# A head's groups in two parts instead of three, and both parts' later steps behind one product

## The chip, the cores and the metric

The kernel runs on one core of one Trainium2 chip. The metric is the device time of one execution in microseconds (us); lower is better. Everything is float32. The matrix products of the model use the reduced form fp32r three times (high part times high, high times low, low times high) to keep the accuracy; the small products of the attention are plain float32.

## The reference, cut to what matters

One encoder layer over 2048 prompt tokens and 64 sample tokens. After an RMS norm one large projection gives ten streams of 1024 columns. Two branches follow: a gated short convolution, and a gated linear recurrence (8 heads, keys and values of 128). The change touches the recurrence alone:

```python
def hgrn2_block(S, q, k, v, logf):          # one chunk of 64 tokens
    b = jnp.cumsum(logf, axis=1)
    ref = b[:, (L - 1) // 2][:, None]
    att = jnp.where(causal, jnp.einsum('bthk,bshk->bhts', q * jnp.exp(b - ref), k * jnp.exp(ref - b)), 0.0)
    o = jnp.einsum('bhts,bshv->bthv', att, v) + jnp.einsum('bthk,bhkv->bthv', q * jnp.exp(b), S)
    S_new = jnp.exp(b_last)[..., None] * S + jnp.einsum('bshk,bshv->bhkv', k * jnp.exp(b_last[:, None] - b), v)
    return S_new, o
...
    o = o * lax.rsqrt(jnp.mean(o * o, axis=-1, keepdims=True) + EPS)
```

The prompt starts from a zero state, the sample from a given one. The outputs are gated, projected, merged with the other branch, normed, and gated once more.

## The kernel before

The 2112 tokens (the 64 sample tokens stand at position 1344) are cut into three blocks of 704. In each block the kernel runs path B (the recurrence, 8 heads), path A (the convolution branch), then the merge and the output layers.

**Products.** The projections are made by `sgroup` (line 328), which replaces two output tiles' eight half-size block products by seven (`PRODUCTS`), each of 12 matmuls: four blocks of the inner dimension times the three fp32r forms (lines 343, 344 and 345; a 128 x 128 weight against 352 tokens). After each product `hook()` (line 238) takes the next entry of a list and runs it. `None` is an empty turn. In the first block the sums of weight blocks and the low parts of all weights are computed on the way by VectorE (DVE) and written to memory; the later blocks load them.

**A head.** `head_prep` (line 720) makes the forget gate and the queries in one group of seven products, the gate z and the values in a second. On the way ScalarE (ACT) and DVE work out the decays: L727 (sigmoid, from the last of the first seven products), L734 (Ln, with the load of its function table), L736, L737 (the running sum), L739, then exponentials (L748 to L750) and L760 to L765, which end in the keys `kb` (L762). The next head's attention reads these.

**The attention.** Tokens of a block go in groups of 128 (two chunks, called pairs here), and one of 64 at the end: five pairs and one single. `plan()` puts them in three parts: four pairs, one pair, one single. `head_attn` (line 781) is a generator with four steps, for one part:

- step 1: transposes of keys and values (L799, L801) into PSUM, copies to SBUF (ACT, L803, L804), scores (L813, L815), masked copies (DVE, L817, L819);
- step 2: the products keys x values (L825), and the chain of states (DVE, L842, one link per group; L846 for a final state);
- step 3: the outputs (L862 and L864), then their norm: square (ACT, L868), sum (DVE, L869), scale (DVE, L527), power -1/2 (GpSimd, L529, inside `rstd_of`), multiply (DVE, L871);
- step 4: transposes of the outputs (L876) and the multiplication with gate and weight into z (DVE, L878).

`path_b` (line 881) puts these steps into the list of hooks, so a head's attention runs between the 14 products of the next head: step 1 of the three parts after products 1, 2 and 3, step 2 after 4, 5 and 6, step 3 after 7, 8 and 9, an empty turn, step 4 after 11, 12 and 13, and the spill of z to memory after 14.

```python
            for step in range(4):
                hooks.extend(partial(next, g) for g in attn)
                if step == 2:
                    hooks.append(None)
            hooks.append(partial(keep_z, hd, d["z"]))
```

The matmuls of a step are placed right behind the last matmul of the product (`placed()`). On the other engines a scheduler that runs when the program is built sets the order; each engine then works through its queue in that order. One pool of three PSUM banks (`psa`, tiles `pa`) serves the attention, another of five (`psg`, tiles `pg`) the products. The tiles of the parts with one group are called `one` (8 buffers of one group); the four-group tiles come from the large ring `r`.

In the first block every head is followed by one more group of seven products (the branch gates, `gates`); in the other two blocks seven of these eight groups have been made before the heads start.

Of the kernel before, what the change touches and what calls it, by code (L numbers as in the profile page):

```python
# [18 lines left out]
P = 128  # L19
# [4 lines left out]
CH = 64  # L24
# [21 lines left out]
def plan():  # L46
# [3 lines left out]
    for t0 in range(0, TOK, BN):  # L50
# [9 lines left out]
        parts = [groups[i : min(i + 4, npair)] for i in range(0, npair, 4)] + [[g] for g in groups[npair:]]  # L60
# [22 lines left out]
def hybrid_step(  # L83
# [697 lines left out]
    def head_attn(ip, gs, d, hd):  # L781

        nt, ln = len(gs), gs[0]["len"]
        o0, n = gs[0]["off"], nt * ln
        qe, z, att = d["qe"], d["z"], atts[ip]

        def tile3():
            if nt == 1:
                return small.tile([P, 1, P], F32, tag="one", name=nm("one"), bufs=8)
            return cols3(rt(nt * P), nt)  # L790

        def keys(g):
            return d["kb"][:, g["off"] : g["off"] + ln]
# [3 lines left out]
        with placed():  # L797
            for i, g in enumerate(gs):
                T.transpose(p_k[:ln, i * P : i * P + P], keys(g), ident)  # L799
            for i, g in enumerate(gs):  # L800
                T.transpose(p_v[:ln, i * P : i * P + P], d["vt"][:, g["off"] : g["off"] + ln], ident)  # L801
        kt, v = tile3(), tile3()
        A.copy(kt[:ln], cols3(p_k, nt)[:ln])  # L803
        A.copy(v[:ln], cols3(p_v, nt)[:ln])  # L804
        p_a = ps_attn()
        with placed():
            for i, g in enumerate(gs):
                o = g["off"]
                if nt > 1:
                    own, rows = d["ka"][:, o // 2 : o // 2 + P], P  # L810
                else:
                    own, rows = d["ka"][:, o // 2 : o // 2 + CH] if ln == P else keys(g), CH
# [4 lines left out]
        V.copy_predicated(att[:CH, :nt, :ln], caus[:CH, :ln].unsqueeze(1).to_broadcast([CH, nt, ln]), pa3[:CH, :, :ln])  # L817
        if ln == P:
            V.copy_predicated(att[CH:, :nt, CH:], caus[CH:, CH:].unsqueeze(1).to_broadcast([CH, nt, CH]), pa3[CH:, :, CH:])  # L819
# [3 lines left out]
        with placed():  # L823
            for i in range(nt):
                T.matmul(p_u[:, i * P : i * P + P], kt[:ln, i, :], v[:ln, i, :], start=True, stop=True)  # L825
        ss = tile3()
        prevs = []
        sample = gs[0]["sample"]
        if sample:
            cur = small.tile([P, P], F32, tag="s0", name=nm("s0"), bufs=2)  # L830
            G.dma_start(cur, s0[hd])
        else:
            cur = states[hd] if d["carry"] is None else d["carry"]
        for i, g in enumerate(gs):
            u = p_u[:, i * P : i * P + P]
            c = (g["off"] + ln) // CH - 1
# [7 lines left out]
        if g["end"]:  # L844
# [378 lines left out]
```

## Time and profile before

| | |
|---|---|
| median of 3 runs | 2762.88 us (2762.08 to 2769.86) |
| profiled execution, its time | 2764.13 us |
| profiled execution, its span | 2761.8 us |
| TensorE matmuls (PE) | 2683.5 us busy, 97% |
| TensorE weight loads (PEld) | 2608.6 us, 94% |
| VectorE (DVE) | 1718.2 us, 62% |
| ScalarE (ACT) | 1449.9 us, 52% |
| GpSimd (POOL) | 377.3 us, 14% |
| granted TensorE clock | 0.987 |

The span is the time from the first to the last instruction; the time of an execution has some 2 us more. A row of the timeline gives the start in us from the start of the span, the duration of the instructions in the row (several that follow each other are one row, with xN), the engine, the line, the operation, the tile written and the tiles read, the shapes, and in square brackets how long the engine stood idle before, and for what. A float32 matmul of the attention shows as two matmuls (x2), a transpose as one. A matmul's duration overlaps the next one's, so the cost of a stretch is read from start to start. Path B's heads run at about 121 to 480 us (first block), 1117 to 1380 us (second) and 1998 to 2290 us (third).

### The profile page before, as it was taken

What the parts mean: (1) busy time and instruction counts of PE and PEld (TensorE: products, weight loads), DVE (VectorE), ACT (ScalarE), POOL (GpSimd) and SP (SyncE); (2) the same over time, 40 slices, a digit from 0 to 9 for tenths busy, and PEclk for the clock granted to TensorE, in tenths of its full rate; (3) what the DMA queues carried; (4) which work ended last, traced back from release to release, by engine and by line L of the source; (5) the groups of instructions that cost most, each with busy time, mean ns of one, the idle gap of its engine ahead of it and who ended that gap; (6) DMA issues with size and microseconds to landing.
All of it is one profiled execution on the core that took longest, in us unless ns stands there. A gap on an engine that the chain in (4) does not pass through costs nothing.

```text
span 2761.8 us, 47890 instructions
## 1 busy us (share of the span) xinstructions
PE 2683.5 (97%) x16736; PEld 2608.6 (94%) x16736; DVE 1718.2 (62%) x3338; ACT 1449.9 (52%) x2796; POOL 377.3 (14%) x698
## 2 busy tenths in 40 slices
PE   6999999999999999999999999999999999999998
PEld 5999999999999999999999999999999999999988
DVE  6788888899657544455645567453355554357764
ACT  4665565454324554566654555454555554445654
POOL 2000001110332211011111210021000000010022
PEclk7999999999999999999999999999999999999999
DMA  5767767888987898766689998599866668888878
GB/s 199 267 237 272 253 240 277 284 308 292 351 314 274 318 320 272 232 210 214 220 271 335 388 336 261 166 358 305 275 210 207 207 218 261 271 287 303 279 234 314
DMA packets 365553, 748.37 MB, mean 271 GB/s; under 512 B 44704, under 2 KB 48320, under 8 KB 365312
## 3 DMA queue, kind: packets, MB, share of 16 engines
q1 hardware_dynamic: 325728, 589.84, 64.3%
q0 software_dynamic: 39296, 155.44, 15.4%
q8 instruction: 132, 2.16, 0.3%
q14 instruction: 109, 0.89, 0.1%
q10 hardware_dynamic: 288, 0.05, 0.0%
HBM read 537.77 MB, written 207.37 MB: 270 GB/s over the span
## 4 chain that ended last, share of the span: by engine, by line
PE 78%; DMA 8%; issue 4%; DVE 4%; POOL 2%; ACT 1%; DVEq 0%; POOLq 0%; ACTq 0%; SPq 0%
PE pg L343 18%; PE pg L344 17%; PE pg L345 17%; PE pg L436 3%; PE pg L437 3%; PE pg L471 3%; PE pg L438 3%; PE pg L469 3%; PE pg L470 3%; DMA raw<-w_blk 2%; DMA raw<-S 1%; PE pa L825 1%; PE pa L862 1%; PE pa L864 1%; DMA r<-w_blk 1%
## 5 line engine op out<-in xcount | busy, mean ns | idle before, releaser
L343 PE MATMUL pg<-r,hi 128*128 128x352 f32 x3360 | 1116.7, 333 | 12.7 <-ACT r L182 5.9
L344 PE MATMUL pg<-r,hi 128*128 128x352 f32 x3360 | 1089.7, 325 | 4.9 <-DVE r L183 4.9
L213 ACT CAST hi<-raw 128x512 fp32r<-128x512 f32 x740 | 456.0, 619 | 633.2 <-PE pg L344 233.2
L345 PE MATMUL pg<-r,lo 128*128 128x352 f32 x2400 | 779.4, 325 | 5.2 <-DMA lo<-low 4.6
L343 PEld LDWEIGHTS pg<-r,hi 128*128 128x128 f32 x3360 | 633.8, 189 | 31.6 <-ACT hf L359 11.3
L344 PEld LDWEIGHTS pg<-r,hi 128*128 128x128 f32 x3360 | 635.4, 189 | 9.5 <-DVE r L183 9.5
L345 PEld LDWEIGHTS pg<-r,lo 128*128 128x128 f32 x2400 | 453.3, 189 | 7.3 <-DMA lo<-low 6.4
L345 PE MATMUL pg<-r,s 128*128 128x352 f32 x960 | 310.9, 324 | 0.6 <-DMA s<-low 0.6
L469 PE MATMUL pg<-r,hi 128*128 128x352 f32 x896 | 290.8, 326 | 2.7 <-ACT r L182 2.4
L470 PE MATMUL pg<-r,hi 128*128 128x352 f32 x896 | 291.6, 326 | 1.3 <-DVE r L183 1.0
L471 PE MATMUL pg<-r,lo 128*128 128x352 f32 x728 | 237.2, 326 | 7.6 <-DVE lo L183 6.2
L182 ACT CAST r<-r 128x352 fp32r<-128x352 f32 (+2 forms) x294 | 162.9, 589 | 143.1 <-DVE r L962 43.7
L182 ACT CAST hi<-raw 128x512 fp32r<-128x512 f32 (+1 forms) x232 | 138.0, 597 | 188.0 <-PE pg L344 51.7
L183 DVE TENSOR_TENSOR r<-r,r 128x352 fp32r<-128x352 f32 (+2 forms) x294 | 183.5, 649 | 61.9 <-ACT r L182 61.1
L183 DVE TENSOR_TENSOR lo<-raw,hi 128x512 fp32r<-128x512 f32 (+1 forms) x232 | 151.7, 657 | 76.6 <-ACT hi L182 66.3
L436 PE MATMUL pg<-r,hi 128*128 128x352 f32 x560 | 183.0, 331 | 9.3 <-ACT r L182 9.3
L437 PE MATMUL pg<-r,hi 128*128 128x352 f32 x560 | 183.9, 329 | 0.8 <-DVE r L183 0.6
L345 PEld LDWEIGHTS pg<-r,s 128*128 128x128 f32 x960 | 180.6, 188 | 1.0 <-DMA s<-low 0.9
L182 ACT CAST hi<-s 128x512 fp32r<-128x512 f32 x160 | 99.0, 619 | 151.8 <-PE pg L344 146.4
L469 PEld LDWEIGHTS pg<-r,hi 128*128 128x128 f32 x896 | 169.6, 190 | 5.0 <-ACT r L182 3.9
L470 PEld LDWEIGHTS pg<-r,hi 128*128 128x128 f32 x896 | 169.8, 190 | 2.8 <-DVE r L183 2.6
L359 ACT COPY hf<-pg 128x352 f32<-128x352 f32 x360 | 158.3, 446 | 0.5 <-PE pg L345 0.5
(317 smaller groups left out, 3985.1 us busy)
## 6 DMA issues: line engine op xcount, KB each, us to landing
raw<-w_blk SPq DMA_DIRECT2D x588, 256.0 KB, 4.0
lo<-low SPq DMA_DIRECT2D x422, 256.0 KB, 3.9
raw<-S SPq DMA_DIRECT2D x400, 256.0 KB, 4.1
low<-lo SPq DMA_DIRECT2D x344, 256.0 KB, 3.5
s<-low SPq DMA_DIRECT2D x318, 256.0 KB, 3.8
S<-s SPq DMA_DIRECT2D x160, 256.0 KB, 3.2
r<-x_fm POOLq DMA_DIRECT2D x40, 352.0 KB, 6.8
r<-w_blk POOLq DMA_DIRECT2D x48, 256.0 KB, 7.1
```

What stands on the lines that cost most here:

```text
L182: A.copy(hi, src)
L183: V.tensor_tensor(lo, src, hi.bitcast(F32), ALU.subtract)
L213: A.copy(hi, raw)
L343: add(hi[:, k, :], xhi, start=start and k == 0, stop=False)
L344: add(hi[:, k, :], xlo, start=False, stop=False)
L345: last[0] = add(lo[:, k, :], xhi, start=False, stop=k == KH - 1).ins
L359: copied = A.copy(got[n], ps[bank])
L436: add(hi[:, k, :], xhi, start=start and k == 0, stop=False)
L437: add(hi[:, k, :], xlo, start=False, stop=False)
L469: T.matmul(ps, hi[:, k % 4, :], xhi[:, c], start=k == 0, stop=False)
L470: T.matmul(ps, hi[:, k % 4, :], xlo[:, c], start=False, stop=False)
L471: last[0] = T.matmul(ps, lo[:, k % 4, :], xhi[:, c], start=False, stop=k == KB - 1).ins
```

## The change

The parts become two: four pairs, and a pair with the single. Step 1 keeps one turn per part (after products 1 and 2). Steps 2, 3 and 4 run for both parts in one turn: after products 4, 6 and 9; z is spilled after product 10, and the list has ten entries instead of fourteen. Inside `head_attn` the work of the second part, whose groups have different lengths, is done with a pair's instructions and a single's: copies, squares, sums, powers and multiplies keep one instruction for the pair and one for the single (`alike`), in that order; the multiplication into z takes both in one instruction of 192 columns. The second part's tiles hold two groups (`two`, 4 buffers), and the two groups share the PSUM tiles, the tile `on` that takes first the squares and then the normed outputs, and the tile `ms` of sums.

The diff:

```diff
@@ -57,7 +57,7 @@
                     groups.append(dict(off=o, len=min(2 * CH, b - o), sample=sample, first=t0 + o == 0, end=o + 2 * CH >= b))
         npair = sum(g["len"] == 2 * CH for g in groups)
         assert all(g["len"] == 2 * CH for g in groups[:npair])
-        parts = [groups[i : min(i + 4, npair)] for i in range(0, npair, 4)] + [[g] for g in groups[npair:]]
+        parts = [groups[i : i + 4] for i in range(0, len(groups), 4)]
         halves = [dict(t0=t0 + o, off=o, n=HN) for o in (0, HN)]
         out.append(dict(t0=t0, n=BN, runs=runs, npair=npair, parts=parts, groups=groups, segs=halves, last=t0 + BN == TOK))
     return out
@@ -780,60 +780,73 @@
 
     def head_attn(ip, gs, d, hd):
 
-        nt, ln = len(gs), gs[0]["len"]
-        o0, n = gs[0]["off"], nt * ln
+        nt, o0, n = len(gs), gs[0]["off"], sum(g["len"] for g in gs)
         qe, z, att = d["qe"], d["z"], atts[ip]
+        pairs = sum(g["len"] == P for g in gs)
 
         def tile3():
-            if nt == 1:
-                return small.tile([P, 1, P], F32, tag="one", name=nm("one"), bufs=8)
+            if nt == 2:
+                return small.tile([P, 2, P], F32, tag="two", name=nm("two"), bufs=4)
             return cols3(rt(nt * P), nt)
 
+        def alike(*tiles):
+
+            out = [tuple(t[:, :pairs] for t in tiles)] if pairs else []
+            return out + ([tuple(t[:CH, pairs:] for t in tiles)] if pairs < nt else [])
+
         def keys(g):
-            return d["kb"][:, g["off"] : g["off"] + ln]
+            return d["kb"][:, g["off"] : g["off"] + g["len"]]
 
 
         p_k, p_v = ps_attn(), ps_attn()
         with placed():
             for i, g in enumerate(gs):
-                T.transpose(p_k[:ln, i * P : i * P + P], keys(g), ident)
+                T.transpose(p_k[: g["len"], i * P : i * P + P], keys(g), ident)
             for i, g in enumerate(gs):
-                T.transpose(p_v[:ln, i * P : i * P + P], d["vt"][:, g["off"] : g["off"] + ln], ident)
+                T.transpose(p_v[: g["len"], i * P : i * P + P], d["vt"][:, g["off"] : g["off"] + g["len"]], ident)
         kt, v = tile3(), tile3()
-        A.copy(kt[:ln], cols3(p_k, nt)[:ln])
-        A.copy(v[:ln], cols3(p_v, nt)[:ln])
+        for dst, src in alike(kt, cols3(p_k, nt)) + alike(v, cols3(p_v, nt)):
+            A.copy(dst, src)
         p_a = ps_attn()
         with placed():
             for i, g in enumerate(gs):
-                o = g["off"]
-                if nt > 1:
+                o, ln = g["off"], g["len"]
+                if ln < P:
+                    own, rows = keys(g), CH
+                elif pairs > 1:
                     own, rows = d["ka"][:, o // 2 : o // 2 + P], P
                 else:
-                    own, rows = d["ka"][:, o // 2 : o // 2 + CH] if ln == P else keys(g), CH
+                    own, rows = d["ka"][:, o // 2 : o // 2 + CH], CH
                 T.matmul(p_a[:rows, i * P : i * P + CH], own, qe[:, o : o + CH], start=True, stop=True)
                 if ln == P:
                     T.matmul(p_a[:, i * P + CH : i * P + P], keys(g), qe[:, o + CH : o + P], start=True, stop=True)
         pa3 = cols3(p_a, nt)
-        V.copy_predicated(att[:CH, :nt, :ln], caus[:CH, :ln].unsqueeze(1).to_broadcast([CH, nt, ln]), pa3[:CH, :, :ln])
-        if ln == P:
-            V.copy_predicated(att[CH:, :nt, CH:], caus[CH:, CH:].unsqueeze(1).to_broadcast([CH, nt, CH]), pa3[CH:, :, CH:])
+
+        def masked(rows, gr, c):
+            dst = att[rows, gr, c]
+            V.copy_predicated(dst, caus[rows, c].unsqueeze(1).to_broadcast(list(dst.shape)), pa3[rows, gr, c])
+
+        if pairs:
+            masked(slice(0, CH), slice(0, pairs), slice(0, P))
+            masked(slice(CH, P), slice(0, pairs), slice(CH, P))
+        if pairs < nt:
+            masked(slice(0, CH), slice(pairs, nt), slice(0, CH))
         yield
 
         p_u = ps_attn()
         with placed():
-            for i in range(nt):
-                T.matmul(p_u[:, i * P : i * P + P], kt[:ln, i, :], v[:ln, i, :], start=True, stop=True)
+            for i, g in enumerate(gs):
+                T.matmul(p_u[:, i * P : i * P + P], kt[: g["len"], i, :], v[: g["len"], i, :], start=True, stop=True)
         ss = tile3()
         prevs = []
-        sample = gs[0]["sample"]
-        if sample:
-            cur = small.tile([P, P], F32, tag="s0", name=nm("s0"), bufs=2)
-            G.dma_start(cur, s0[hd])
-        else:
-            cur = states[hd] if d["carry"] is None else d["carry"]
         for i, g in enumerate(gs):
+            if g["sample"]:
+                cur = small.tile([P, P], F32, tag="s0", name=nm("s0"), bufs=2)
+                G.dma_start(cur, s0[hd])
+            else:
+                cur = states[hd] if d["carry"] is None else d["carry"]
             u = p_u[:, i * P : i * P + P]
-            c = (g["off"] + ln) // CH - 1
+            c = (g["off"] + g["len"]) // CH - 1
             if g["first"]:
                 prevs.append(None)
                 V.tensor_copy(ss[:, i, :], u)
@@ -841,23 +854,23 @@
                 prevs.append(cur)
                 V.scalar_tensor_tensor(ss[:, i, :], cur, d["f"][:, c : c + 1], u, ALU.mult, ALU.add)
             cur = ss[:, i, :]
-        if g["end"]:
+            if not g["end"]:
+                d["carry"] = cur
+                continue
             end = small.tile([P, P], F32, tag="state", name=nm("state"), bufs=NH + 2)
             V.tensor_scalar(end, cur, d["eq"][:, c * CH + CH - 1 : c * CH + CH], None, ALU.mult)
-            if sample:
+            if g["sample"]:
                 G.dma_start(hgrn_s[hd], end)
             else:
                 states[hd] = end
                 if d["last"]:
                     G.dma_start(hgrn_p[hd], end)
-        else:
-            d["carry"] = cur
         yield
 
         p_o = ps_attn()
         with placed():
             for i, g in enumerate(gs):
-                o = g["off"]
+                o, ln = g["off"], g["len"]
                 dst = p_o[:ln, i * P : i * P + P]
                 T.matmul(dst, att[:ln, i, :ln], v[:ln, i, :], start=True, stop=prevs[i] is None)
                 if prevs[i] is not None:
@@ -865,15 +878,17 @@
         on = tile3()
         ms = small.tile([P, 4], F32, tag="ms", name=nm("ms"))
         po3 = cols3(p_o, nt)
-        A.activation(on[:ln], po3[:ln], AF.Square)
-        V.tensor_reduce(ms[:ln, :nt], on[:ln], axis=mybir.AxisListType.X, op=ALU.add)
-        rstd_of(ms[:ln, :nt], ms[:ln, :nt], 1.0 / P)
-        V.tensor_tensor(on[:ln], po3[:ln], ms[:ln, :nt].unsqueeze(2).to_broadcast([ln, nt, P]), ALU.mult)
+        for dst, src, m in alike(on, po3, ms[:, :nt]):
+            A.activation(dst, src, AF.Square)
+            V.tensor_reduce(m, dst, axis=mybir.AxisListType.X, op=ALU.add)
+            rstd_of(m, m, 1.0 / P)
+            V.tensor_tensor(dst, src, m.unsqueeze(2).to_broadcast(list(dst.shape)), ALU.mult)
         yield
         p_t = ps_attn()
         with placed():
-            for i in range(nt):
-                T.transpose(p_t[:, i * ln : i * ln + ln], on[:ln, i, :], ident[:ln, :ln])
+            for i, g in enumerate(gs):
+                o, ln = g["off"] - o0, g["len"]
+                T.transpose(p_t[:, o : o + ln], on[:ln, i, :], ident[:ln, :ln])
         c = slice(o0, o0 + n)
         V.scalar_tensor_tensor(z[:, c], p_t[:, :n], g_on[:, hd : hd + 1], z[:, c], ALU.mult, ALU.mult)
         yield
@@ -890,11 +905,13 @@
             next(fills, None)
             assert not hooks
             attn = [head_attn(i, gs, d, hd) for i, gs in enumerate(bl["parts"])]
-            for step in range(4):
-                hooks.extend(partial(next, g) for g in attn)
-                if step == 2:
-                    hooks.append(None)
-            hooks.append(partial(keep_z, hd, d["z"]))
+
+            def both(attn=attn):
+                for g in attn:
+                    next(g)
+
+            hooks.extend(partial(next, g) for g in attn)
+            hooks.extend((None, both, None, both, None, None, both, partial(keep_z, hd, d["z"])))
 
 
     def load_p(bl, queue):
```

In the program as built, the matmuls outside the attention stand in the same order as before, and every engine has the same instructions but for 25 fewer on DVE (the multiplication into z, and one memset). The single's square now waits for the pair's multiply, since both use the tile `on` and the PSUM tile. In seven heads of the first block the scheduler put the transpose of the single 33 matmuls behind the transposes of the pairs; in the other 17 heads all six transposes stand together.

## The prediction

> **What bounds the kernel now.** I read the page first, then the busy times of the three stretches of heads, then PE's list of waits.
>
> ```profile
> span 2761.8 us, 47890 instructions
> PE 2683.5 (97%) x16736; PEld 2608.6 (94%) x16736; DVE 1718.2 (62%) x3338; ACT 1449.9 (52%) x2796; POOL 377.3 (14%) x698
> 121.00:480.00 359.00, 357.75 (x2312) 343.07 (x2311) 301.75 (x604) 203.98 (x387) 31.94 (x48) 1.00 0.73 257
> 1117.00:1380.00 263.00, 263.00 (x1738) 250.24 (x1737) 149.99 (x353) 155.79 (x295) 29.36 (x49) 1.00 0.67 216
> 1998.00:2290.00 292.00, 292.00 (x1925) 277.63 (x1924) 161.90 (x371) 165.59 (x316) 26.80 (x43) 1.00 0.68 212
> PE pa L801 <- ACT one L803: 1.5, 1, 1.5
> PE pa L799 <- ACT one L803: 1.4, 1, 1.4
> ```
>
> In the stretches (window; its length; then busy PE, PEld, DVE, ACT, POOL; clock; DMA) PE is busy without a hole: 357.75 of 359 us, 263 of 263, 292 of 292, at full clock. So the heads cost what PE's queue costs, and an edit can help only by making that queue shorter or by removing one of PE's few waits. Of the waits, two belong to the attention, 1.5 and 1.4 us, each once. The change can lose by new waits: PE works in order, so a late operand stops everything behind it. DVE is busy for 301.75 us of the first block's 359 (84%), and for 57% (149.99 of 263) in the second: the first block has little room to be late.
>
> **PE's own work.** The number of attention matmuls is unchanged; seven interruptions of the products per head go. What does an interruption cost?
>
> ```profile
> 1221.81 0.33 PE L345 MATMUL pg<-r,s 128*128 128x352 f32 x1
> 1221.97 0.27 PE L876 MATMUL pa<-ident,one 128*128 128x128 f32 x1
> 1222.00 0.41 PE L343 MATMUL pg<-r,hi 128*128 128x352 f32 x1
> 1222.25 0.33 PE L344 MATMUL pg<-r,hi 128*128 128x352 f32 x1
> ...
> 1235.55 0.32 PE L345 MATMUL pg<-r,s 128*128 128x352 f32 x1
> 1235.71 0.27 PE L799 MATMUL pa<-ident,r 128*64 128x128 f32 x1
> 1235.82 0.27 PE L801 MATMUL pa<-ident,r 128*64 128x128 f32 x1
> 1236.02 0.33 PE L813 MATMUL pa<-r,r 128*64 128x64 f32 x2
> 1236.28 0.43 PE L343 MATMUL pg<-r,hi 128*128 128x352 f32 x1
> 1236.55 0.32 PE L344 MATMUL pg<-r,hi 128*128 128x352 f32 x1
> ```
>
> Read from start to start, a matmul of a product takes 0.16 us (1221.81 to 1221.97). One full transpose between products moves the second matmul behind it to 1222.25, that is 0.44 us after 1221.81 where two matmuls alone take 0.32: 0.12 us. The same operation inside a row of its kind takes 0.11 (1235.71 to 1235.82). So an interruption as such costs 0.01 us, since the 0.25 at its end (1222.00 to 1222.25) is given back by the 0.03 before it. 168 interruptions fewer (7 x 24 heads) bring 0 to 2 us; I take 1.
>
> The 64-wide pieces do cost a change: the scores of the single start 0.20 after the transpose ahead of them instead of 0.11 (1235.82 to 1236.02). The merged step 1 has two such places, as the two clusters have now: the pair's narrow L813 and the single's. In steps 2 to 4 the single's 64-row matmuls keep one way in and one way out. I take 0, between 1 us less and the bound of the second rival.
>
> [...]
>
> The two waits of 1.5 and 1.4 us are the third part's transposes waiting for the second part's copies on ACT; that turn is empty now, and step 2 comes a product later: 2.9 us less.
>
> **The new lateness: the single's norm.** Step 3 to step 4 was four products and is now three. And the single's norm no longer runs beside the pair's: its square waits for the pair's multiply, so square, sum, scale, power and multiply run twice in a row. I work it out from one head of the first block, with time 0 at the start of the square of the four pairs.
>
> ```profile
> 343.96 0.39 PE L864 MATMUL pa<-r,r 128*128 128x128 f32 x2
> ...
> 348.59 0.43 PE L862 MATMUL pa<-one,att 64*64 64x128 f32 x2
> ...
> 349.31 0.43 PE L343 MATMUL pg<-r,hi 128*128 128x352 f32 x1
> ```
>
> PE: the last output matmul of the four pairs starts at 344.07 (second half of the row at 343.96), 0.32 before time 0 (row 344.39 below). Then the pair's four halves (0.11 each, 0.45), the single's way in (0.20) and its work (0.72, 348.59 to 349.31): the next product starts 1.36 after 344.07. Three products are 36 x 0.16, with 0.09 more at the first: 5.85. So the transposes start 7.2 after 344.07, at 6.9. In blocks two and three the single's comes behind five others (0.54) and its way in (0.1): needed at 7.55. In seven heads of the first block 33 matmuls stand between (5.3, with 0.2 at both ends): needed at 12.9.
>
> ```profile
> 342.83 0.52 DVE L383 TENSOR_TENSOR hf<-hf,pg 128x352 f32<-128x352 f32 x1 [0.31 <-PE pg L345]
> 343.38 0.50 ACT L727 ACTIVATE r<-hf 128x352 f32<-128x352 f32 x1
> 344.39 0.60 ACT L868 ACTIVATE r<-pa 128x512 f32<-128x512 f32 x1 [0.51 <-PE pa L864]
> 345.69 1.28 ACT L734 ACT_TABLE_LOAD   x1
> 346.51 0.16 DVE L527 TENSOR_SCALAR ms<-ms 128x4 f32<-128x4 f32 x1
> 346.82 1.04 POOL L529 TENSOR_TENSOR ms<-ms,mhalf 128x4 f32<-128x4 f32 x1 [20.85 <-DVE ms L527]
> 346.98 0.98 ACT L734 ACTIVATE r<-r,lbt 128x704 f32<-128x704 f32 x1
> 347.90 0.69 DVE L871 TENSOR_TENSOR r<-pa,ms 128x512 f32<-128x512 f32 x1 [1.22 <-POOL ms L529]
> 348.50 0.64 DVE L736 TENSOR_SCALAR r<-r,lbt 128x704 f32<-128x704 f32 x1
> 349.06 1.62 DVE L737 TENSOR_TENSOR_SCAN r<-keep,r 128x704 f32<-128x704 f32 x1
> 350.59 1.26 DVE L183 TENSOR_TENSOR lo<-raw,hi 128x512 fp32r<-128x512 f32 x2
> 351.78 0.88 DVE L739 TENSOR_TENSOR r<-r 128x704 f32<-128x704 f32 x1
> 352.58 0.46 DVE L869 TENSOR_REDUCE ms<-one 128x1 f32<-128x128 f32 x2
> 352.97 0.67 DVE L183 TENSOR_TENSOR lo<-s,hi 128x512 fp32r<-128x512 f32 x1
> 353.57 0.20 DVE L527 TENSOR_SCALAR ms<-ms 128x1 f32<-128x1 f32 x2
> 353.69 0.67 DVE L279 TENSOR_TENSOR s<-s,raw 128x512 f32<-128x512 f32 x1
> 355.31 0.28 DVE L871 TENSOR_TENSOR one<-pa,ms 64x128 f32<-64x128 f32 x1 [0.20 <-POOL ms L529]
> 362.38 0.73 DVE L878 SCALAR_TENSOR_TENSOR r<-pa,vec,r 128x512 f32<-128x512 f32 x1
> ```
>
> The four pairs' multiply ends at 4.2, as before (347.90 + 0.69 - 344.39). Behind it in the built order stand the pair's L527 and L383 (0.52, on the seventh product, which now follows step 3): 4.7.
>
> Blocks two and three: scale to multiply takes 1.39 with a power of 1.04 (346.51 to 347.90); for the two small groups, one after the other, it takes 1.74 (353.57 to 355.31), so 0.9 is taken for one. The pair is multiplied from 5.0 to 5.3; then the single's square (taken as 0.3, as its sum and multiply), sum 0.3, scale to multiply 0.9, multiply 0.3: 7.0 to 7.1. Needed at 7.55: hidden, with 0.5 us to spare, behind the three products. I take 0. If each of the chain's ten hand-overs takes 0.1 longer, it costs 0.5 in each of the 16 heads.
>
> First block: L727 (0.50) waits for L383 and the Ln's table load (1.28) and Ln (0.98) follow: Ln ends at 7.5, where it ended at 3.6 before (346.98 + 0.98 - 344.39). On DVE the built order behind it is L736, L737, two L183, the single's sum, L739, L183, the single's scale, the four pairs' L878, L279, the single's multiply. From start to start in the rows: 0.56, 1.53, 1.19, 0.20, 0.80, 0.60, 0.08, 0.66, 0.60 and 0.28 for the last: 6.5. The multiply ends at 14.1, the transpose wants it at 12.9: PE stands for about 1.25 us, queued behind it the rest of the product and all later ones. In seven heads 8.8 us. The ends are 0 (if Ln comes a microsecond earlier) and 2.2 a head (15 us; if a cast that a L183 waits for is late by one more).
>
> **What else is late.** The exponentials and the keys follow Ln. In the first block seven gate products still stand between (84 matmuls, 13 us) and cover the 3.9 us. In blocks two and three the keys are done well ahead:
>
> ```profile
> 1261.26 0.48 DVE L762 TENSOR_TENSOR r<-hf,qc 128x320 f32<-128x320 f32 x1
> 1265.39 0.60 PE L799 MATMUL pa<-ident,r 128*128 128x128 f32 x4
> ```
>
> 3.65 us. The three output steps that stood behind the seventh product (3.1 us of PE: 16 halves at 0.11 and the 1.36 worked out above) now stand ahead of it, and Ln comes about as long after that product as before. By that 0.5 us is left. Hidden, at 0; without that cover each microsecond costs 16. Step 3 after step 2 is two products (3.9 us) and the chain of six states takes some 2 us: hidden. The spill of z is issued earlier on POOL, behind nothing that it waited for before.
>
> **Sum.** -1 (interruptions) + 0 (mode changes) - 2.9 (two waits) + 8.8 (first block) + 0 (blocks two and three) = +4.9. The profiled execution took 2764.1 (span 2761.8 and 2.3 around it), 1.25 above the median 2762.9 of the runs; with the change 2769.0 by the profile, 2768 against the median. What a measurement of this kernel can tell from no change is about 0.3%, 8.3 us: so I forecast no change that can be told, on the slow side.
>
> **Rivals.**
>
> *The serial norm is late in every head* (slower). Place: the single's transpose. If the chain is 1 us longer than worked out, blocks two and three lose 0.5 in 16 heads (8) and the first block 2.25 in seven (16): +20, 2783. It passes 8.3 us from a lengthening of 0.5 us: 7 x 1.75 - 3.9. For it: ten hand-overs between four engines, and DVE's 84%. Against: the durations repeat from head to head. 0.22.
>
> *Each change of tile width drains* (slower). Step 1 would go to narrow tiles and back once more. One such trip costs 0.24: from 1235.55 to 1236.55 is 1.00, less two matmuls of a product (0.32) and the four pieces at 0.11 (0.44). 0.24 x 24 = 5.8 on top: +10.7, 2774. Against: row 1235.71, a 64-wide transpose that starts 0.16 behind a full matmul, and the next 0.11 behind it, so transposes pay nothing. [...] 0.08.
>
> *An interruption costs a fixed price* (faster). If the 0.09 of the first matmul behind each (0.25 instead of 0.16) were a net cost, 168 fewer save 15 us: 2753. Against: the 0.12 worked out above. [...] 0.05.
>
> *The change does nothing that shows*: no head waits, as the scheduler left 33 matmuls for it. -3.9: 2759. 0.20.
>
> **Numbers.** Forecast 0.45, of it 0.36 inside 0.3% and 0.09 above. Same: 0.36 + 0.18 (nothing shows; 0.02 of it faster) + 0.04 (norm late) + 0.02 = 0.60. Slower: 0.09 + 0.18 + 0.06 = 0.33. Faster: 0.02 + 0.05 = 0.07. The range goes from 2757 (no new waits, the two old ones gone, 2 less for interruptions, and a margin of 1 us) to 2781 (15 us in the first block, 6 in the others, less 3).
>
> **What would show it.** PE waits in the first block at the transpose of the single (tile `two`) for DVE's multiply, seven times about 1.2 us; none in blocks two and three; the two waits for L803's copies gone; clusters as long as their parts were. It is wrong if PE has waits at the pairs' transposes, at step 2 or 3, or at the next head's first transposes, or if the products between clusters are no longer 0.16 apart.

## The result, and the profile after

The change makes the kernel slower. Its median is 2778.97 us (2776.59 to 2783.8, six runs) against 2762.82 (2761.1 to 2769.86, six runs) of the kernel before: a ratio of 1.0056, 95% interval 1.0043 to 1.0069. That is 16 us, inside the range of 2757 to 2781, but twice the 8.3 us (0.3%) that the prediction took as the bound of what can be told, and had forecast it to stay under. The profiled execution took 2783.8 us, 19.7 more than that of before; its span is 20.3 longer.

Two rows of the page after, for the span and the engines:

```profile
span 2782.1 us, 47864 instructions
PE 2686.9 (97%) x16736; PEld 2623.0 (94%) x16736; DVE 1721.9 (62%) x3313; ACT 1452.6 (52%) x2796; POOL 374.7 (13%) x698
```

No engine has more work to speak of. The busy times by stretch (columns as in the prediction) show where the time is: first before, then after.

```profile
150.00:500.00 350.00, 347.27 (x2239) 332.94 (x2238) 295.85 (x598) 196.26 (x374) 32.07 (x49) 1.00 0.74 260
```

```profile
150.00:500.00 350.00, 329.42 (x2065) 318.38 (x2066) 279.30 (x547) 184.06 (x343) 24.50 (x39) 0.98 0.71 240
1140.00:1420.00 280.00, 280.00 (x1851) 269.04 (x1850) 157.90 (x370) 163.10 (x314) 30.70 (x51) 1.00 0.68 217
2030.00:2310.00 280.00, 280.00 (x1839) 269.21 (x1838) 160.50 (x358) 160.66 (x301) 26.60 (x43) 1.00 0.66 210
```

In blocks two and three PE is busy without a hole, as before. The loss is in the first block's heads: PE stands still for 20.6 of 350 us there (2.7 before), and the granted clock is 0.98. PE's waits in the first block's heads (what waits, for what; total us, times, longest) are two rows:

```profile
PE pg L343 <- DVE hf L364: 13.6, 7, 2.0
PE pa L891 <- DVE two L885: 7.5, 7, 1.1
```

The second row is the wait that the prediction priced: the single's transpose, seven times. The first row is new and was not in it. L364 is an addition on DVE that reads a bank of the products' PSUM pool; until it has run, the bank isn't free and the next product of the gate group can't start. The two waits for the copies of the old L803 are gone.

### The profile page after: what moved, and what is told of

Read it like the earlier page. It is cut to its first block, busy times and chain, and to the rows that moved or that the text cites. A ratio compares the mean times of both kernels' runs of the same rounds, so it can differ in the third digit from the quotient of the medians.

```text
span 2782.1 us, 47864 instructions
## 1 busy us (share of the span) xinstructions
PE 2686.9 (97%) x16736; PEld 2623.0 (94%) x16736; DVE 1721.9 (62%) x3313; ACT 1452.6 (52%) x2796; POOL 374.7 (13%) x698
## 4 chain that ended last, share of the span: by engine, by line
PE 79%; DMA 6%; DVE 5%; issue 4%; POOL 1%; ACT 1%; DVEq 0%; POOLq 0%; SPq 0%; ACTq 0%
PE pg L343 18%; PE pg L344 18%; PE pg L345 18%; PE pg L436 3%; PE pg L437 3%; PE pg L438 3%; PE pg L471 3%; PE pg L469 3%; PE pg L470 3%; DMA raw<-w_blk 2%; DMA lo<-low 2%; PE pa L839 1%; PE pa L875 1%; PE pa L877 1%; PE pa L820 1%
## 5 line engine op out<-in xcount | busy, mean ns | idle before, releaser
L343 PE MATMUL pg<-r,hi 128*128 128x352 f32 x3360 | 1106.8, 330 | 23.6 <-DVE hf L364 13.6
L183 DVE TENSOR_TENSOR r<-r,r 128x352 fp32r<-128x352 f32 (+2 forms) x294 | 183.5, 649 | 62.3 <-ACT r L182 61.4
L183 DVE TENSOR_TENSOR lo<-raw,hi 128x512 fp32r<-128x512 f32 (+1 forms) x232 | 151.9, 658 | 81.0 <-ACT hi L182 71.6
```

The source lines that it names most:

```text
L183: V.tensor_tensor(lo, src, hi.bitcast(F32), ALU.subtract)
L343: add(hi[:, k, :], xhi, start=start and k == 0, stop=False)
```

## Where the new wait comes from

One head of the kernel after (timeline; rows as explained above): rows of ACT and DVE first, then rows of PE.

```profile
362.24 0.98 ACT L734 ACTIVATE r<-r,lbt 128x704 f32<-128x704 f32 x1
...
368.19 0.73 DVE L893 SCALAR_TENSOR_TENSOR r<-pa,vec,r 128x512 f32<-128x512 f32 x1
369.45 0.28 DVE L885 TENSOR_TENSOR two<-pa,ms 64x128 f32<-64x128 f32 x1
370.46 0.41 DVE L893 SCALAR_TENSOR_TENSOR r<-pa,vec,r 128x192 f32<-128x192 f32 x1
...
376.41 0.88 DVE L765 TENSOR_TENSOR r<-r,qc 128x704 f32<-128x704 f32 x1
377.81 0.51 DVE L364 TENSOR_TENSOR hf<-hf,pg 128x352 f32<-128x352 f32 x1
```

```profile
358.65 0.32 PE L345 MATMUL pg<-r,lo 128*128 128x352 f32 x1
369.78 0.27 PE L891 MATMUL pa<-ident,two 64*128 64x64 f32 x1 [1.08 <-DVE two L885]
378.47 0.40 PE L343 MATMUL pg<-r,hi 128*128 128x352 f32 x1 [1.93 <-DVE hf L364]
```

The same points before, on PE and on DVE:

```profile
342.47 0.32 PE L345 MATMUL pg<-r,lo 128*128 128x352 f32 x1
361.94 0.32 PE L343 MATMUL pg<-r,hi 128*128 128x352 f32 x1
```

```profile
359.94 0.50 DVE L364 TENSOR_TENSOR hf<-hf,pg 128x352 f32<-128x352 f32 x1
360.97 0.87 DVE L765 TENSOR_TENSOR r<-r,qc 128x704 f32<-128x704 f32 x1
362.38 0.73 DVE L878 SCALAR_TENSOR_TENSOR r<-pa,vec,r 128x512 f32<-128x512 f32 x1
```

Time is counted from the start of the last matmul of the seventh product (342.47 before, 358.65 after); 97 matmuls later PE comes to the bank.

- *PE is earlier.* Before, it reaches the bank at 19.47 (361.94). After, at 17.89 (378.47 less 1.93 of waiting): the 22 pieces of the outputs that stood in this stretch now stand ahead of the seventh product, and only the 1.08 at the single's transpose has come in.
- *DVE is later.* Before, L364 ends at 17.97 (359.94 + 0.50), 1.5 us ahead of PE. After, it ends at 19.67 (377.81 + 0.51), 1.8 behind. Ln isn't the cause: it ends at 4.57 after (362.24 + 0.98), where it ended at 5.49 before (346.98 + 0.98 in the prediction's rows). From Ln's end to L364's end DVE needs 15.1 us instead of 12.5. Both multiplications into z and L765 stand ahead of L364 in the built order, where they stood behind it: 1.8 us, from start to start. So do four more operations on the weights, two of L183 and two of L279: 2.3 us. Against them the norms' operations and DVE's own waiting are 1.5 us less.

So 1.5 us to spare became a wait of 1.9. All seven heads have these times to within 0.1 us.

**The wait costs more than its length.** PE behind the same wait in the next head, which lasted 1.95:

```profile
432.18 0.40 PE L343 MATMUL pg<-r,hi 128*128 128x352 f32 x1 [1.95 <-DVE hf L364]
...
432.93 0.49 PE L344 MATMUL pg<-r,hi 128*128 128x352 f32 x1
433.22 0.49 PE L345 MATMUL pg<-r,lo 128*128 128x352 f32 x1
...
436.38 0.32 PE L344 MATMUL pg<-r,hi 128*128 128x352 f32 x1
```

For some 3.5 us the matmuls start 0.29 apart instead of 0.16: the granted clock is 0.50 there (rows of the windows below). Five of the seven waits for L364 are followed by such a stretch, 11 or 12 slow matmuls each, 7.5 us in all; none of the seven waits of 1.1 us is. The five stretches of half clock begin at 159.79, 214.40, 323.63, 432.85 and 487.47 us, last 3.41 us each, and lie 16, 32, 32 and 16 times 3.413 us apart. So in this trace the clock changes at the edges of windows of 3.413 us, and these do not move with PE's waits. Two of these windows and the one behind each, first around the wait at 432.18, then around that at 378.47:

```profile
429.44:432.85 3.41, 1.46 (x9) 1.20 (x9) 3.41 (x7) 1.64 (x3) 0.00 (x0) 1.00 0.76 248
432.85:436.26 3.41, 3.41 (x14) 3.41 (x13) 2.29 (x6) 1.04 (x3) 0.00 (x0) 0.50 0.73 184
374.83:378.24 3.41, 1.71 (x11) 1.41 (x9) 3.41 (x7) 2.53 (x4) 0.00 (x0) 1.00 0.90 338
378.24:381.65 3.41, 3.18 (x20) 3.21 (x21) 3.34 (x8) 1.15 (x3) 0.00 (x0) 1.00 0.76 171
```

The first wait lies whole in one window: PE is busy for 1.46 of its 3.41 us, and the next window has the clock of 0.50. The second is cut by an edge into 1.70 and 0.23, and the clock stays at 1.00.

The sum of the profiled execution: waits for L364 +13.6, slow matmuls behind them +7.5, waits at the single's transpose +7.5, waits for L803 -2.9, interruptions -2.0 (below): +23.7. The span grew by 20.3. Compared at the start of the same matmul of a product, the execution after is 2.7 us ahead before the first attention step (at 119 us) and 23.2 behind past the first block's heads (at 557 us). That is +25.9 in these heads; the terms that fall there give 25.4 (13.6 + 7.5 + 7.5, less 1.5 for L803, 1.0 for five waits for L390 that before has, and 0.7 for a third of the interruptions). So most of the 3.4 that the sum is too high was gained before the change acts, and the change does not explain it.

## The experiments

Each ratio is to the kernel before, timed beside the run (2760.92 to 2761.95 us there). Theory A stands for "VectorE's queue and the place of the outputs", B for "two parts and grouped steps cost TensorE itself"; the other letters are explained in the expectations, where they stand.

**1. L364 first.**

```diff
-                V.tensor_tensor(u2, u2, ps["b"], ALU.add)
+                with tc.high_priority():
+                    V.tensor_tensor(u2, u2, ps["b"], ALU.add)
```

> The changed kernel with one edit: the addition of line 364, which frees a bank of PSUM for the next group of products, is given high priority, so that it stands in VectorE's order behind the first multiply of the outputs instead of behind the keys' and queries' scaling (18 instructions earlier). Theory A (VectorE's order: seven times 2.1 us of the loss are TensorE's wait for that bank, seven times 1.1 us its wait for the single's norm): the waits for line 364 go, -14.7 us; the single's multiply gets up to 1.1 us later in each of the seven heads, 0 to +7.7 us; so 2764 to 2772 us against 2779, ratio to before 1.0005 to 1.0035. Rival B (two parts and steps behind one product cost TensorE time of their own, and the wait at the bank is only where it shows): 2776 to 2780 us, ratio 1.005 to 1.006, the wait shows elsewhere.

2768.86 us, ratio 1.0021 (1.0012 to 1.0031), inside A's range. Its waits in the first block's heads:

```profile
PE pg L343 <- DVE r L391: 7.8, 7, 2.2
PE pa L892 <- DVE two L886: 7.0, 7, 1.0
```

The wait for L364 is gone, and B with it. But a wait of 0.9 has come up (once 2.2) for the next reader of a bank in the same queue, L390 (391 here). The single's wait did not grow, as A had allowed for; but in this program its transpose stands 40 matmuls of the products behind the pairs', 7 more than in the change. With each edit the scheduler places it anew.

**2. Norms abreast.**

```diff
-        for dst, src, m in alike(on, po3, ms[:, :nt]):
+        norms = alike(on, po3, ms[:, :nt])
+        for dst, src, m in norms:
             A.activation(dst, src, AF.Square)
+        for dst, src, m in norms:
             V.tensor_reduce(m, dst, axis=mybir.AxisListType.X, op=ALU.add)
...
```

> The changed kernel with the norms of pair and single written abreast (both squares, both reductions, both powers, both multiplies) instead of one chain after the other. Theory A (one queue: the single's late chain and line 364's late addition both come from VectorE's full order after its idle time for the logarithm): the waits at the single's transpose go, -8.2 us, and as its last links and the multiplies of the outputs now fill the 1.5 us in which VectorE was idle, the addition of line 364 comes 1.5 to 2.5 us earlier and most of its wait goes too, -10 to -14.7 us; so 2756 to 2762 us, ratio 0.9975 to 1.000. Rival C (the serial chain costs its own wait alone; the bank's wait hangs on the logarithm, which is late because the products of the outputs go ahead of the seventh product): -8.2 us alone, 2771 us, ratio 1.003, seven waits of about 2 us for line 364 remain. Rival B (two parts and grouped steps cost TensorE itself): 2776 to 2780 us.

2767.43 us, ratio 1.0015 (1.0007 to 1.0024).

```profile
PE pg L343 <- DVE hf L364: 11.6, 7, 1.8
PE pg L343 <- DVE r L390: 1.9, 7, 0.3
```

The waits at the single's transpose are gone, though it now stands right behind the pairs', without the 33 matmuls between: the serial chain was their cause. L364 still comes late, 1.66 on average instead of 1.94. A missed (2756 to 2762), and C is nearer, with 11.5 us gained instead of its 8.2. The half clock adds to the gain: these waits, 1.59 to 1.76 us, have no slow matmuls behind them.

Why so little of the wait went is seen in one head:

```profile
350.50 0.32 PE L345 MATMUL pg<-r,lo 128*128 128x352 f32 x1
368.20 0.52 DVE L364 TENSOR_TENSOR hf<-hf,pg 128x352 f32<-128x352 f32 x1
368.87 0.40 PE L343 MATMUL pg<-r,hi 128*128 128x352 f32 x1 [1.65 <-DVE hf L364]
```

L364 ends at 18.22 behind the seventh product, 1.45 earlier than in the change, as A had it. But PE comes to the bank at 16.72, 1.2 earlier, since it no longer waits on the way. Before, L364 ended at 17.97 and PE came at 19.47. So in this run the wait is almost all PE's shorter way (2.75 us) and hardly DVE's lateness (0.25). C's reason, a late logarithm, fits this run (Ln ends at 6.75) but not the change (4.57).

**3. Both edits.**

> The changed kernel with both edits: line 364's addition given high priority and the norms of pair and single written abreast. Alone the first left seven waits of 1.1 us for the next addition of the same group (line 391 there) beside the single's 1.0, the second left 7 x 1.7 us for line 364. Theory A (one queue of VectorE that is late by a fixed amount behind the logarithm; whichever of its results is needed first is waited for): the single's wait goes, that for line 364 goes, and some of that for line 391 stays, 4 to 9 us: 2760 to 2766 us, ratio 0.9995 to 1.0015. Rival D (the two waits are separate and each edit takes away its own in full): -14.7 - 8.2 us, 2756 us, ratio 0.998.

2774.94 us, ratio 1.0049 (1.0037 to 1.0061): worse than either alone, and both theories missed.

```profile
PE pg L343 <- DVE r L391: 15.5, 7, 2.3
```

L390 (391 here) ends some 20.7 behind the seventh product, 0.2 later than in six of the seven heads of run 1. But PE comes to its bank 1.1 earlier than there, since the single's wait is gone, and so waits 2.2 instead of 0.9. In total PE waits hardly longer than in run 1 (15.5 against 7.8 + 7.0). What makes this run slower is that the wait is now in one piece: the trace has five stretches of half clock in these heads, that of run 1 one, that of run 2 none. At some 1.5 us each that is the 6 us to run 1, and most of the 7.5 to run 2. The gains of the two edits in one queue did not add: 10.1 and 11.5 us alone, 4.0 together.

**4. Three parts, grouped like the change.** The kernel before, with this list:

```diff
-            for step in range(4):
-                hooks.extend(partial(next, g) for g in attn)
-                if step == 2:
-                    hooks.append(None)
-            hooks.append(partial(keep_z, hd, d["z"]))
...
+            hooks.extend(partial(next, g) for g in attn)
+            hooks.extend((both, None, both, None, None, both, partial(keep_z, hd, d["z"])))
```

> The kernel before with its three parts kept, and only the state updates, outputs and output transposes of all three each behind one product, at the products where the changed kernel has them (4, 6 and 9). Every part has tiles of its own, so the single's norm doesn't follow the pair's. Theory A (the place of the outputs and VectorE's order): line 364 stands behind line 765 in VectorE's order as in the changed kernel, so seven waits of 1.5 to 2.5 us for that bank appear, +10 to +17 us, and none at the single's transpose; less about 1 us for interruptions saved: 2771 to 2779 us, ratio 1.003 to 1.006. Rival B' (the merging into two parts brings the loss, by its serial norm and shared tiles): 2760 to 2766 us, ratio 0.999 to 1.001.

2791.23 us, ratio 1.0100 (1.0087 to 1.0114), above both ranges.

```profile
PE pg L343 <- DVE hf L364: 23.1, 7, 3.3
```

No wait at the single's transpose, and 3.3 us at each bank, every one followed by slow matmuls. L364 ends as late as in the change (19.9 behind the seventh product), and PE, which has not waited on the way, comes at 16.7. So the merging into two parts is not what loses at the bank; the place of the steps is. At these places two parts are 12 us faster than three.

**5. Two parts, each step behind a product of its own** (keys 1 and 2, state updates 4 and 5, outputs 7 and 8, transposes 11 and 12).

> The changed kernel's two parts, but each step of each part behind a product of its own: keys 1 and 2, state updates 4 and 5, outputs 7 and 8, transposes 11 and 12. The serial norm stays. Theory A (place and grouping of the outputs): the outputs are behind the seventh product again, the logarithm isn't late, line 364 stands 8 instructions ahead of line 765, the transposes come 9 us behind the outputs: neither wait; the two waits for the copies of line 803 are gone too, -3.2 us: 2757 to 2763 us, ratio 0.998 to 1.000. Rival B' (the merging brings the loss): 2774 to 2780 us, ratio 1.004 to 1.006, waits at the single's transpose and the bank stay.

2770.79 us, ratio 1.0034 (1.0021 to 1.0047), between the two ranges.

```profile
PE pa L891 <- DVE two L885: 8.8, 7, 1.3
```

The bank is free in time; the single's transpose is late by 1.26. A missed there: it had counted on the 9 us between outputs and transposes. In the trace the single's transpose stands apart from the pair's, eleven matmuls of the products later (it starts at 363.84, the pair's at 360.53, in one head), where the scheduler put it; its operand comes 1.3 us later still.

**6. The same, norms abreast.** The edits of 5 and 2 together.

> The two parts with each step of each part behind a product of its own (which came out at 1.0034 of before, with 7 x 1.26 us of waits at the single's transpose and none for line 364), and the norms of pair and single abreast as the only further edit. Theory A (that version's loss is the serial norm alone): -8.8 us, 2757 to 2763 us, ratio 0.9985 to 1.0005, no waits at the single's transpose. Line 364 goes 6 places back in VectorE's order by this, to the place it has in the version with outputs behind 7, transposes behind 11 and norms abreast, where TensorE did not wait for it. Rival H (VectorE's order is full, and any gain at the norm comes back as a wait for a bank): waits for lines 364 or 773 of 1 us or more, 2766 us or more, ratio above 1.0015.

2759.42 us, ratio 0.9990 (0.9981 to 0.9999). What is left of waits in the first block's heads is 3 us, with one stretch of half clock behind the last two:

```profile
PE pg L343 <- DVE r L390: 1.5, 7, 0.2
PE pa L804 <- ACT r L809: 1.0, 1, 1.0
PE pa L820 <- DVE att L827: 0.5, 1, 0.5
```

A holds: the loss of 5 was the serial norm. This version has two parts and loses nothing, so two parts as such cost nothing.

**7. Outputs behind 7, transposes behind 11.** The change with `(None, both, None, None, both, None, None, None, both, ...)`.

> The changed kernel with the outputs of both parts behind product 7 instead of 6 and the transposes behind 11 instead of 9; the serial norm stays. Theory A (the loss comes from the outputs being ahead of the seventh product, and from three products between outputs and transposes): the logarithm is ready in time, line 364 stands eight instructions ahead of line 765, the single has four products: neither wait, 2757 to 2762 us, ratio 0.998 to 1.000. Rival E (the serial norm costs 7 x 1.2 us wherever it is put, as it did with each step behind a product of its own): 2766 to 2770 us, ratio 1.0015 to 1.003, waits at the single's transpose stay.

2771.77 us, ratio 1.0034 (1.0022 to 1.0046).

```profile
PE pa L891 <- DVE two L885: 13.8, 7, 2.0
```

The bank is free (A's half); the single's wait is longer (E, with 2.0 instead of its 1.2, and a time above its range). The outputs behind the seventh product give PE its longer way to the bank back. The rows of the pair's transpose and the single's:

```profile
362.60 0.27 PE L891 MATMUL pa<-ident,two 128*128 128x128 f32 x1
364.88 0.27 PE L891 MATMUL pa<-ident,two 64*128 64x64 f32 x1 [2.01 <-DVE two L885]
```

Here the single's transpose stands right behind the pair's, where the change has 33 matmuls between. One more product (12 matmuls) stands ahead of them: in all 21 matmuls less, 3.4 us at 0.16 each. The serial norm is only 2.4 us shorter: its multiply ends 11.6 after the start of the four pairs' square, instead of 14.0. The 1.0 left over comes on top of the wait of 1.1, and makes it 2.0.

**8. Outputs behind 7, transposes behind 10.**

> The changed kernel with outputs and transposes one product later, behind 7 and 10: the three products between them stay, and so does the place of line 364 in VectorE's order, behind lines 764 and 765. Only the logarithm comes earlier, by the time of the outputs' products (3.9 us by the trace). Theory A (the lateness of the logarithm, not the order, makes the bank late): the waits for line 364 fall from 2.1 to 0 to 0.6 us each, that of the single from 1.1 to 0 to 1.1: 2757 to 2768 us, ratio 0.998 to 1.002. Rival F (the order alone decides, the idle 1.5 us of VectorE don't matter): 2775 to 2781 us, ratio 1.0045 to 1.0065, both waits as they were.

2818.0 us, ratio 1.0202 (1.0189 to 1.0216): far outside both. The waits of all heads:

```profile
PE pa L891 <- DVE two L885: 40.1, 23, 2.2
```

```profile
1246.99 0.29 DVE L885 TENSOR_TENSOR two<-pa,ms 128x128 f32<-128x128 f32 x1 [0.73 <-POOL ms L529]
1247.20 0.64 DVE L736 TENSOR_SCALAR r<-r,lbt 128x704 f32<-128x704 f32 x1
1247.75 1.62 DVE L737 TENSOR_TENSOR_SCAN r<-keep,r 128x704 f32<-128x704 f32 x1
1249.29 0.25 DVE L883 TENSOR_REDUCE ms<-two 64x1 f32<-64x128 f32 x1
1251.05 0.28 DVE L885 TENSOR_TENSOR two<-pa,ms 64x128 f32<-64x128 f32 x1 [0.65 <-POOL ms L529]
```

At the bank 0.4 us a head is left, put down to ACT, so order alone (F) does not decide: L364 stands behind L765 here too, and the outputs' 22 pieces, with the 2.2 us that PE waits on the way, nearly suffice. But the single's wait is now in the heads of blocks two and three as well, and fourteen stretches of half clock follow the 23 waits: 40.1 us and some 21 more. In the second block's head above, L736 and L737 (2.1 us from start to start) stand between pair and single, since Ln is ready in time. In the same block of the kernel after, Ln comes later and the single goes first:

```profile
1202.43 0.28 DVE L885 TENSOR_TENSOR two<-pa,ms 64x128 f32<-64x128 f32 x1 [0.65 <-POOL ms L529]
1203.61 0.65 DVE L736 TENSOR_SCALAR r<-r,lbt 128x704 f32<-128x704 f32 x1 [0.90 <-ACT r L734]
```

**9. Outputs behind 7, transposes behind 11, norms abreast.** Edits 7 and 2.

> The outputs of both parts behind product 7, the transposes behind 11, and the norms of pair and single abreast. Theory A: with neither wait left, what remains of the change is the two waits for line 803's copies gone (-3.2 us) and some 2 us of interruptions: 2756 to 2760 us, ratio 0.9975 to 0.9995, the fastest of these. Rival (something of the merging itself costs in TensorE): 2764 us or more, ratio above 1.001.

2760.21 us, ratio 0.9993 (0.9985 to 1.0002), 0.2 us above A's range in time and inside it in the ratio. Both waits are gone; small ones for other readers remain:

```profile
PE pg L343 <- ACT hf L359: 3.5, 4, 0.9
PE pg L343 <- DVE r L773: 2.6, 3, 1.1
```

**10. That, with L773 first** (high priority for the two instructions that make the gate).

> Two parts, outputs behind product 7, transposes behind 11, norms abreast, as in the version that came out at 0.9993 of before, and the two instructions of the gate values at and above line 773 (the second reads a bank of PSUM) given high priority: in VectorE's order line 773 comes up 2 places, ahead of the second multiply of the outputs. That version's trace had three waits for line 773, 2.6 us, and four for the copies of line 359, 3.5 us, in the first block's heads. Theory A: the waits for line 773 go, -2 to -3 us: 2755 to 2759 us, ratio 0.998 to 0.999. Rival: the wait passes to the next addition in the order (line 390), 2759 to 2763 us, ratio 0.9993 to 1.0005.

2758.43 us, ratio 0.9988 (0.9979 to 0.9997). The wait for L773 shrank to 0.4 us and one of 0.4 for L390 came up in each head (3.1 in all), too short to matter: the time is A's, the passing on is the rival's. With run 6 this is the fastest version, 2 to 3 us below the kernel before: both intervals lie below 1, but barely.

**11. That of 9, with high priority for every reader of a bank** (L364, L376 to L390, L773).

> As the run beside it, but with high priority for every addition or copy that reads a bank of the products (lines 364, 376 to 383, 385 to 390 and 773). In VectorE's order line 364 comes up 8 places and the first multiply of the outputs goes behind the keys' scaling; line 773 goes 3 places down. Theory A (one queue: what one reader gains the others lose): no wait for line 364, waits for line 773 or 390 of 0.5 to 1.5 us in the seven heads: 2758 to 2766 us, ratio 0.9985 to 1.0015. Rival (all readers early frees all banks): 2753 to 2757 us, ratio below 0.998.

2791.04 us, ratio 1.0108 (1.0094 to 1.0122), outside both.

```profile
PE pa L824 <- DVE att L831: 20.7, 7, 4.7
```

The banks of the products are free in time. But the masked copies (L827, here 831), which have no priority, come late, and they free the banks of the attention's pool: the next scores (L820, here 824) wait for them, up to 4.7 us.

**12. Three parts at 4, 7 and 11.** Run 4 with both later steps moved.

> The kernel before with its three parts, state updates, outputs and transposes of all three each behind one product, but at products 4, 7 and 11 instead of 4, 6 and 9 (which cost 29 us). Theory A (the place of the outputs ahead of the seventh product makes the bank late, not the number of parts nor the grouping): line 364 stands five instructions ahead of where it was in VectorE's order and the logarithm isn't late; no waits for it, 2758 to 2765 us, ratio 0.999 to 1.0015. Rival G (grouping three parts floods VectorE wherever it is put): waits of 2 us and more stay, each followed by products at half clock in about half the cases: 2775 us or more, ratio above 1.005.

2776.16 us, ratio 1.0052 (1.0040 to 1.0065): inside G's range.

```profile
PE pg L343 <- DVE r L773: 13.8, 7, 2.9
```

L364 is in time, as A had it; another reader, L773, behind L765 and all three multiplications into z, is 2 us late, as G had it; three of the seven waits have slow matmuls behind them. In both runs grouping makes a burst of DVE work, and its place decides which reader is caught in it: L364 in run 4 (up to 3.3 us), L773 here (up to 2.9).

## Why the prediction was right and wrong

- *PE's queue sets the time; no work is added.* Right: PE's busy time (2683.5 us before, 2686.9 after) and its clock in blocks two and three (1.00) are as before.
- *Interruptions, -1.* Right. From start to start, all stretches of attention matmuls cost 243.9 us before (288 stretches; 2.8 of it waits) and 246.6 after (127; 7.5 of it waits), over the products' own 0.16 each: 241.1 and 239.1 without waits, -2.0 for 161 interruptions fewer (in seven heads the single's transpose stands apart). The rival with a fixed price (-15) is out. So is the rival with a drain at each change of width (+5.8), which no run shows: the merged step 1 costs 1.52 us a head, where the pair's and the single's clusters cost 0.90 and 0.68 before.
- *Waits for L803, -2.9.* Right.
- *The single's norm, +8.8.* Right, a little large. Its multiply was worked out to end at 14.1 and ended 14.0 after the start of the square; PE waits 1.02 to 1.10 seven times, 7.5 where 8.8 was taken. Run 2 shows that the serial chain is the cause.
- *Blocks two and three, 0.* Right, by little, as run 8 shows.
- *"What else is late", 0.* This step failed. It followed the late Ln to its last product, the keys, and found 13 us of cover. It did not ask what else stands in the same DVE queue behind that chain. The readers of the products' banks do, and each has its own time at which PE wants it. The margin of L364 was there to read, 1.5 us before; the step put at nothing what measured 13.6 us of waits and 7.5 of slow matmuls behind them. The step also named the outputs ahead of the seventh product as what makes Ln late, and did not see the other side of that move: they no longer stand between that product and the bank, and PE arrives 1.6 us earlier.
- *The price of a wait* was taken as its length. Five of the seven waits of 1.9 us cost 1.5 us more.

The rival "serial norm late in every head" had +20 in its sum, near the profile's +20.3, by another mechanism: no head of blocks two and three waits. The list of what would show the prediction wrong did not hold the case either: the wait stands inside a group of products, at none of the places named.

The reading with which runs 2, 4, 7 and 8 were set out, that a late Ln makes the bank late, fell for the change: behind the seventh product Ln is earlier there than before (4.57 against 5.49). What the runs bear out is the pair above, PE's shorter way and DVE's fuller queue, 1.6 and 1.7 of the 3.3 us. The two are not independent: the 1.1 us that PE waits at the single's transpose is part of its way to the bank. Where that wait is gone, PE comes at 16.7, and the bank's wait stays even with DVE nearly as early as before (run 2). Where PE's way is long again and the norms are abreast, it is gone (runs 6 and 9).

## What to carry to other kernels

When work moves past an instruction, follow both sides: who is late behind it, and who arrives earlier because the moved work no longer stands in its way. On an engine that works through one queue and is 80% busy (DVE here, 279.30 of 350 us), list everything that another engine waits for, with its time to spare, not only the chain that the change touches; relieving one entry shifted the wait to the next (run 1: 0.9 us for L390), and a wait taken away brought the waiting engine earlier to the next one (run 2: PE 1.2 us). And price a wait of the matrix engine at its length only where it is short: in this kernel two waits of 1 us cost less than one of 2 (run 1 against run 3: 14.8 and 15.5 us of waits, 2768.86 and 2774.94 us).

## What the runs showed of the hardware

In the heads' stretches of the 14 traces (116 to 544, 1140 to 1420 and 2030 to 2310 us), none of 82 waits of PE between 0.34 and 1.68 us was followed by half clock by itself; two of them together, 0.98 and 0.50 us in run 6, were. Of 49 between 1.69 and 2.32 us, 32 were: mostly 12 matmuls at 0.29 instead of 0.16 us, 1.55 us more. All 14 of 2.58 us and more were. The same wait in the same kernel has the slow stretch in one head and not in the next (1.93 and 1.95 above), by where the edge of a window falls.

Laid on the windows of 3.413 us that the clock's own changes mark in each trace, 47 windows of these stretches at full clock were followed by half clock, and in 46 of them PE stood idle for 1.69 us or more. Of the 3990 that were followed by full clock, 5 had as much. So in these runs half a window of idle time (1.69 of 3.413 us) parts the two kinds, but for six windows.

If a window that is idle for half its length counts, a wait of 2.0 us falls so in 2.0/3.413 = 59% of the cases, an estimate from the windows measured here; the runs had 32 of 49, 65%.
